# Gated-merge blocks staged in f32 in a later block's place, their split spaced by matmul columns, and the second gate's weights split ahead of the conv forms

## The chip, the core and the metric

One core of one Trainium2 chip runs the whole encoder block in one launch. The metric is the device time of the program in microseconds (us), as the median of repeated runs. The engines are called by the profile's names: PE is TensorE's matmul queue, PEld its weight loads, DVE is VectorE, ACT is ScalarE, POOL is GpSimd, and SP (SyncE) issues every DMA of the part that is told here. Each engine takes its instructions in the order of its own queue; semaphores tie the queues together.

## The reference, cut to what matters

```
u = RMSNorm(x)
[q|k|v|cB|cC|cH|gA|gB] = u @ W_in               # gA, gB: 1024 channels each
A   = neighbourhood_attention(q, k, v)          # 512 channels
B   = cB * conv3(cC * cH)                       # 512 channels
y_A = A @ W_A ;  y_B = B @ W_B                  # to 1024 channels each
m   = sigmoid(gA) * y_A + sigmoid(gB) * y_B     # per channel and token
x   = x + m @ W_o
x   = x + relu(RMSNorm(x) @ W1)^2 @ W2
```

There are 1024 tokens and 1024 channels, all in float32.

## The kernel before

Every f32 operand of a matmul is scaled by a power of two and split into two f16 halves, `hi` (ACT: a scaled copy) and `lo` (DVE: the scaled operand minus `hi`). A product is then three f16 matmuls. The scale of a weight chunk comes from its squares or its largest entry. ACT or DVE makes one column per chunk, DVE rounds it to bf16 (`sum_of`, L1173 and L1174, or `largest`, L389 and L391), PE sums it over the partitions with a 128x1 matmul on `ones` (`all_sum`, L231), and DVE reads the sum back (L234) and makes the scale with some five one-column operations (`pow2_half`, L490 to L497, or `pow2`). A chunk's column sum here always means that 128x1 matmul: it stands in PE's queue between products, so everything behind it waits until DVE has cast the column.

The change lies in the middle of the program, between the attention and the output projection. There the merged activations m are made in eight blocks n of 128 channels:

- Gate n (`gate_units`): the two gates' products for block n. For n from 1 to 7 they are made by a seven-product scheme (`seven`): seven units of 12 matmuls on sums of the weights' quarters ("forms", `gsum`, made by POOL in `forms_sum`, L1320) and on sums of the activations (`FORM`). A gate's four 512-token pieces live in a tile `sg`, of which there are two. The posts of a unit add the products into `sg` on DVE (L1463 to L1480), and one ACT sigmoid (L1474) ends the gate.
- Attention units (`a_unit`): one unit of 12 matmuls for half the tokens of a block; DVE multiplies the product into `sg` (L1515).
- Conv units (`ab`): blocks n = 2j and 2j+1 share seven units of 6 matmuls on forms of the conv branch. Those activations' forms are made once (`conv_late`: `hi`, L938; `lo`, L941), parked in `M`, written to DRAM (`bf`) and read back form by form into four slots (`land`, tile `bT`). DVE multiplies the products into `sg` (L1526).
- `join` adds both halves of a block on POOL (L1536); when both 512-token halves are in, `m_done` squares the block (ACT, L1436), makes a scale (DVE, L1438 and L490 to L497) and splits it into the two halves of `M` (ACT L1441, DVE L1443). `M` is a pair of tiles of eight blocks each, `mH` and `mL`, and is what the output projection reads.

The weights of gate n are prepared by `prep_s(n)` (tile `w_s`: ACT L1338 for `hi`, DVE L1334 for `lo`), those of the conv branch by `prep_b(j)` (`w_wb`, same lines), those of the attention branch by `prep` (`w_wa`, L362 and L349). The raw weights come through five buffers (`raw`, L264 on SP), each loaded again when its last reader is through.

The order of all this on the engines is made when the program is built. `unit` writes a unit's matmuls and then advances background work: `tick` steps the list `bg` (weight preparations), `step` steps `fg` (forms, splits of m). A preparation spaces its own steps by `apart`, which waits until a number of matmul columns (`work`; one unit of 12 is 6144) has been written. `built` drives both lists until a chunk's weights are split.

```
def apart(mark, n=3, of=units):
    while of[0] < mark + n and not forced[0]:
        yield WAIT
```

Of the kernel before, what the change touches and what calls it, by code (L numbers as in the profile page):

```python
# [101 lines left out]
def encoder_block(ctx: ExitStack, tc: tile.TileContext, x, weights, cols, gqk, rel, masks, out):  # L102
# [28 lines left out]
    area = {"keep": [0, 0, 144], "prep": [144, 144, 240], "tmp": [240, 240, 512]}  # L131
# [814 lines left out]
    def conv_late():  # L946

        zs = zb.rearrange("p n t -> p (n t)").bitcast(F16).rearrange("p (n w t) -> p n w t", n=4, w=2)
        ms = [M[i][:, 2 + n].rearrange("p (w t) -> p w t", w=2) for i in range(2) for n in range(6 - 2 * i)]
# [236 lines left out]
    def aged(ch, i):  # L1186
        return forced[0] or i >= len(ch.when) or work[0] >= ch.when[i] + 2 * 6144
# [154 lines left out]
    def forms_split(ch, t, s, P):  # L1342
# [6 lines left out]
        todo = [(0, 1, r[0][:, 0:1]), (1, 3, r[1]), (3, 5, t[:, 0:2]), (5, 7, t[:, 2:4])]  # L1349
        yield from parts([((lambda i, a=a, b=b: P[:, a:b, i]), w) for a, b, w in todo], s, then)  # L1350
# [3 lines left out]
    def prep_s(n):  # L1354
# [6 lines left out]
        else:  # L1361
            yield from rows_scaled(ch, g1)
            sm = yield from squares(ch, M[1][:, 7].bitcast(BF16))
# [15 lines left out]
    def prep_b(j):  # L1379
# [7 lines left out]
        for a in range(2):  # L1387
            A.activation(M[1][:, 6, :512].bitcast(BF16), raw[:, 512 * a:512 * a + 512], AF.Square,
# [40 lines left out]

    def m_done(n):  # L1430

        m = sgs[n][:, 0::2]
        hi, lo = (M[w][:, n].rearrange("p (h t) -> p h t", h=2) for w in range(2))
        ss, s = tmp(), tmp()
        yield
        A.activation(lo.bitcast(BF16), m, AF.Square, accum_out=sc[:, ss])  # L1436
        yield
        V.tensor_scalar(sc[:, ss], sc[:, ss], 1e-36, None, op0=OP.max)  # L1438
        yield
        yield from pow2_half(ss, 14, s, at(rowsM, n))  # L1440
        A.activation(hi, m, AF.Copy, scale=sc[:, s])  # L1441
        yield
        V.scalar_tensor_tensor(lo, m, sc[:, s], hi, op0=OP.mult, op1=OP.subtract)  # L1443
        merged.add(n)

    def gate_units(n, tail=None):
# [24 lines left out]
        def post3(ps):  # L1471
# [3 lines left out]
            if tail:  # L1475
                tail(sg, 0)
        seven(cS[n].P, actS, 0, 512, {
            1: lambda ps: A.activation(z[0], ps[1], AF.Copy),
            6: lambda ps: V.tensor_tensor(z[1], ps[6], z[0], op=OP.add),
            2: lambda ps: V.tensor_tensor(z[0], ps[2], z[0], op=OP.add),  # L1480
            5 if n == 1 else 7: post7, 3: post3}, 2, 5 if n < 7 else 6, (1, 6, 2, 4, 7, 5, 3) if n == 1 else (1, 6, 2, 4, 5, 7, 3))
# [795 lines left out]
```

## Time and profile before

| | |
|---|---|
| median of 3 runs (lowest to highest) | 1222.78 us (1222.61 to 1223.08) |
| the profiled execution's own time | 1222.02 us |
| span of its profile | 1220.2 us |
| mean granted PE clock | 0.994 |
| PE busy | 1191.6 us, 98% of the span |
| DVE busy | 959.1 us, 79% |
| ACT busy | 777.6 us, 64% |
| POOL busy | 479.9 us, 39% |

Times in the rows of the profile are us from the start of the span. A row of the timeline gives the start, the length, the engine (with q for its sequencer), the line of the kernel, the operation, what is written and read, and in brackets how long the engine had been idle before it and what released it. The chip's DMA engines carry out what SP issues: a DMA row on SP is the issue, not the transfer.

### The profile page before, as it was taken

How to read it: one execution, taken by the hardware profiler on the slowest of the kernel's cores; microseconds unless marked ns; L12 is line 12 of the kernel's file. 1: busy time of each engine (PE TensorE's matmuls, PEld its weight loads, DVE VectorE, ACT ScalarE, POOL GpSimd, SP SyncE). 2: the span in 40 equal slices, each digit the busy share in tenths (PEclk: the TensorE clock that was granted, in tenths of full speed). 3: DMA queues.
4: the chain of work that ended last, by engine and by line, in shares of the span. 5: the costliest groups of instructions: out<-in, count | busy, mean ns of one | idle time of the engine just before them, and what ended most of it. 6: DMA issues, size and time to landing. Idle time of an engine off the chain costs nothing.

```text
span 1220.2 us, 17138 instructions
## 1 busy us (share of the span) xinstructions
PE 1191.6 (98%) x6248; PEld 573.6 (47%) x6248; DVE 959.1 (79%) x1793; ACT 777.6 (64%) x1241; POOL 479.9 (39%) x314
## 2 busy tenths in 40 slices
PE   8999999999897998999999999999999999999998
PEld 7444444545343443444458444444444444444444
DVE  7987778898787867876878665555448989999998
ACT  7775668778665745335768887687776754646430
POOL 5610021121433341401003665755657563464472
PEclk9999999999899999999999999999999999999999
DMA  7755555777583423316096654354384934436212
GB/s 264 201 152 114 110 112 116 154 157 136 140 303 126 154 71 121 104 71 258 18 176 153 207 190 148 137 190 153 133 293 164 345 129 156 174 113 231 96 43 104
DMA packets 168373, 189.62 MB, mean 155 GB/s; under 512 B 123616, under 2 KB 124128, under 8 KB 164192
## 3 DMA queue, kind: packets, MB, share of 16 engines
q1 hardware_dynamic: 168288, 188.52, 51.4%
q8 instruction: 49, 0.80, 0.3%
q14 instruction: 36, 0.29, 0.1%
HBM read 117.19 MB, written 41.42 MB: 130 GB/s over the span
## 4 chain that ended last, share of the span: by engine, by line
PE 79%; DVE 12%; ACT 4%; POOL 2%; issue 2%; DMA 2%; DVEq 0%; ACTq 0%; POOLq 0%
PE ps_d L240 23%; PE ps_s L240 19%; PE ps_o L240 17%; PE ps_d L1161 10%; DVE w_s L1334 2%; PE ps_d L690 2%; PE ps_d L739 2%; PE ps_s L739 2%; DVE w_wb L1334 2%; PE ps_s L690 1%; PE ps_o L1142 1%; PE ps_s L1066 1%; DMA raw<-in_weights 1%; POOL sg L1536 1%; DVE sc L381 1%
## 5 line engine op out<-in xcount | busy, mean ns | idle before, releaser
L240 PEld LDWEIGHTS <-ops 128*128 128x128 f16 x1356 | 132.5, 98 | 157.3
L240 PEld LDWEIGHTS <-w 128*128 128x128 f16 x1368 | 132.8, 98 | 139.5
L1161 PE MATMUL ps_d<-uT,w_ws 128*128 128x512 f16 x576 | 127.9, 379 | 0.0
L240 PE MATMUL ps_s<-ops 128*128 128x512 f16 (+1 forms) x528 | 119.7, 377 | 0.0
L240 PE MATMUL ps_d<-ops 128*128 128x512 f16 x480 | 110.1, 379 | 0.0
L2098 ACT ACTIVATE ops<-hf,sc 128x2048 f16<-128x2048 f32 x26 | 52.0, 1998 | 84.8 <-PE ps_s L240 37.7
L1320 POOL TENSOR_TENSOR tsum<-raw 128x512 f32<-128x512 f32 x28 | 48.2, 1740 | 139.4 <-DVE v L1726 74.7
L1676 POOL TENSOR_TENSOR as<-as 128x512 f32<-128x512 f32 x60 | 83.0, 1383 | 41.6 <-ACT as L1958 38.0
L240 PEld LDWEIGHTS <-w_s 128*128 128x128 f16 x588 | 57.8, 100 | 87.1 <-issue 16.2
L1161 PEld LDWEIGHTS <-w_ws 128*128 128x128 f16 x576 | 54.5, 98 | 65.1 <-issue 1.0
L240 PE MATMUL ps_d<-u2T,w 128*128 128x512 f16 (+1 forms) x360 | 78.8, 368 | 0.0
L240 PE MATMUL ps_o<-ops 128*128 128x512 f16 (+1 forms) x348 | 78.6, 375 | 0.0
L2100 DVE SCALAR_TENSOR_TENSOR ops<-hf,sc,ops 128x2048 f16<-128x2048 f32 x26 | 74.2, 2852 | 3.2 <-ACT ops L2098 2.2
L240 PE MATMUL ps_o<-u2T,w 128*128 128x512 f16 (+1 forms) x348 | 76.0, 368 | 0.0
L240 PE MATMUL ps_s<-u2x,w 128*128 128x512 f16 (+1 forms) x336 | 74.5, 371 | 0.0
L1196 ACT ACTIVATE raw<-raw,sc 128x256 f32<-128x256 f32 x164 | 67.8, 494 | 7.2 <-DMA raw<-in_weights 7.2
L1536 POOL TENSOR_TENSOR sg<-sg 128x512 f32<-128x512 f32 x14 | 20.4, 1466 | 95.7 <-DVE sg L1515 55.6
L1338 ACT ACTIVATE w<-raw,sc 128x512 f16<-128x512 f32 (+1 forms) x28 | 24.6, 927 | 50.5 <-DVE sc L496 50.5
L1991 DVE TENSOR_TENSOR as<-ps_s,as 128x512 f32<-128x512 f32 x13 | 9.0, 692 | 57.9 <-ACT as L2010 57.9
L2114 POOL TENSOR_TENSOR raw<-raw 128x1024 f32<-128x1024 f32 x8 | 30.8, 3873 | 36.8 <-DVE ops L2108 36.8
L240 PEld LDWEIGHTS <-mH 128*128 128x128 f16 x304 | 29.6, 98 | 30.8 <-issue 0.3
L2104 ACT ACTIVATE ops<-raw,sc 128x1024 f16<-128x1024 f32 x24 | 26.3, 1138 | 26.6 <-DVE sc L152 19.2
(429 smaller groups left out, 2734.6 us busy)
## 6 DMA issues: line engine op xcount, KB each, us to landing
raw<-in_weights SPq DMA_DIRECT2D x89, 512.0 KB, 5.8
hs<-as SPq DMA_DIRECT2D x16, 1792.0 KB, 7.9
hf<-hs SPq DMA_DIRECT2D x26, 1024.0 KB, 6.4
bT<-bf SPq DMA_DIRECT2D x28, 512.0 KB, 4.9
w2x<-in_weights SPq DMA_DIRECT2D x16, 512.0 KB, 7.6
raw<-in_weights SPq DMA_DIRECT2D x16, 384.0 KB, 3.6
xt<-in_x SPq DMA_DIRECT2D x8, 512.0 KB, 10.6
gs<-s SPq DMA_DIRECT2D x4, 1024.0 KB, 4.5
```

Source lines behind the costliest of these rows:

```text
L240: T.matmul(ps, l, r, start=a, stop=b)
L690: T.matmul(ps, UT[:, sa, k, b * 128:(b + 1) * 128], w, start=(kind, k) == ("hh", 0), stop=(kind, k) == ("hl", 7))
L739: T.matmul(vbank["q", b], UT[:, sa, k, b * 128:(b + 1) * 128], cQ.parts[:, sw, 512 * k:512 * k + 512], start=(k, n) == (0, 0), stop=(k, n) ...
L1161: T.matmul(ps, l, r, start=a, stop=b)
L1196: A.activation(v, v, AF.Copy, scale=sc[:, at(g, 4 * i + k)])
L1320: G.tensor_tensor(t[:, o], a, b, op=OP.add)
L1334: V.scalar_tensor_tensor(o(1), w, sc[:, scale(n - 1)], o(0), op0=OP.mult, op1=OP.subtract)
L1536: G.tensor_tensor(t, t, part(n, 2 * half + 1), op=OP.add)
L1676: sub.tensor_tensor(z[o], z[a], z[b], op=op)
L2098: A.activation(P[:, 1, 0], hf, AF.Copy, scale=sc[:, Rs])
L2100: V.scalar_tensor_tensor(P[:, 1, 1], hf, sc[:, Rs], P[:, 1, 0], op0=OP.mult, op1=OP.subtract)
L2114: G.tensor_tensor(w11[i2], w11[i2], w12[i2], op=OP.add)
```

## The change

1. A finished block n below 6 is no longer joined in `sg`. POOL writes the sum in f32 to `whole(n)`: two neighbouring 1024-column places of `mH` (even n) or `mL` (odd n), those of blocks n+1 and n+2, which are written later. So `sg` is free after the joins, and the two loops that stepped until block n-2 was split, ahead of a gate, are gone.
2. `m_done` reads that place and spaces its four steps (square, scale, `hi`, `lo`) one unit (6144 columns) apart, and it waits for the block before it. Scale columns are kept (`sums`, `scales`) and not taken from a ring. A loop before the output projection forces what is left.
3. The weights of gate 1 are put ahead of the conv forms and of `prep_b(0)` in the lists, without the wait of a unit, and with the last two pairs of forms in the other order. Gate 1's units run in the order 1, 2, 6, 4, 7, 5, 3 (before 1, 6, 2, 4, 7, 5, 3).
4. `built` first tries up to 12 plain steps before it forces. The first raw weights of gate 2 are used 4 units after their load, not 2.
5. Scratch outputs of squares move from `mL` to `mH`, and the parking of the conv forms is spread 5 and 5 over `mH` and `mL` (it was 6 and 4).

```diff
@@ built
+        for _ in range(12):
+            if all(ch.split for ch in chs):
+                return
+            tick()
+            step()
         forced[0] = True
...
@@ aged
-        return forced[0] or i >= len(ch.when) or work[0] >= ch.when[i] + 2 * 6144
+        return forced[0] or i >= len(ch.when) or work[0] >= ch.when[i] + (4 if ch is cS[2] else 2) * 6144
...
@@ prep_s, forms_split
+        if turned:
+            todo[2:] = todo[:1:-1]
...
-        yield from apart(work[0], 6144, work)
+        if n > 1:
+            yield from apart(work[0], 6144, work)
...
-        yield from forms_split(ch, t, s, ch.P)
+        yield from forms_split(ch, t, s, ch.P, n == 1)
...
+    def whole(n):
+        return M[n % 2][:, n + 1:n + 3].rearrange("p n t -> p (n t)").bitcast(F32)
...
@@ m_done
+        if n < 6:
+            m, gap = whole(n), 6144
+        else:
+            m, gap = sgs[n][:, 0::2], 0
+            hi, lo = (t.rearrange("p (h t) -> p h t", h=2) for t in (hi, lo))
+        while n and n - 1 not in merged:
+            yield WAIT
+        yield from apart(work[0], gap, work)
         A.activation(lo.bitcast(BF16), m, AF.Square, accum_out=sc[:, ss])
         yield
+        yield from apart(work[0], gap, work)
         V.tensor_scalar(sc[:, ss], sc[:, ss], 1e-36, None, op0=OP.max)
         yield
+        s = at(scales, n)
         yield from pow2_half(ss, 14, s, at(rowsM, n))
+        yield from apart(work[0], gap, work)
         A.activation(hi, m, AF.Copy, scale=sc[:, s])
         yield
+        yield from apart(work[0], gap, work)
         V.scalar_tensor_tensor(lo, m, sc[:, s], hi, op0=OP.mult, op1=OP.subtract)
...
@@ join
-            G.tensor_tensor(t, t, part(n, 2 * half + 1), op=OP.add)
+            o = whole(n)[:, 512 * half:512 * half + 512] if n < 6 else t
+            G.tensor_tensor(o, t, part(n, 2 * half + 1), op=OP.add)
...
@@ the order of the stage
     tick(8)
+    bg.append(prep_s(1))
+    tick(2)
     fg.append(first_forms())
-    bg.extend([prep_b(0), prep_s(1)])
+    bg.append(prep_b(0))
...
             built(cS[n])
-            while j and n - 2 not in merged:
-                step()
             sgs[n] = gate_units(n)
...
         settle()
-        while n - 2 not in merged:
-            step()
         sgs[n] = gate_units(n)
```

What moves is shown at three places. Rows of the kernel before carry its line numbers; those of the changed kernel stand 5 to 31 lines further on for the same code.

First, ACT's queue from the split of the first attention weights (`w_wa`) on, at the start of this stage. `w_s` are the split weights of gate 1, `zb`, `mH` and `mL` from `bT` are the conv forms' `hi`, and `sg` from `raw` and `ps_o` are the sigmoids of gate 0. Before:

```order
L362 ACTIVATE w_wa<-raw,sc 128x256 x4
L938 ACTIVATE zb<-bT 128x512 x3
L1388 ACTIVATE mL,sc<-raw,sc 128x512 x2
L1196 ACTIVATE raw<-raw,sc 128x2x128 x4
L938 ACTIVATE mH<-bT 128x512 x3
L1457 ACT_TABLE_LOAD
L1457 ACTIVATE sg<-raw 128x512
L1454 ACTIVATE sg<-ps_o,sc 128x512
L938 ACTIVATE zb<-bT 128x512
L938 ACTIVATE mH<-bT 128x512
L1338 ACTIVATE w_s<-raw,sc 128x512
```

The same stretch of ACT's queue now:

```order
L367 ACTIVATE w_wa<-raw,sc 128x256 x4
L1343 ACTIVATE w_s<-raw,sc 128x512
L1343 ACTIVATE w_s<-raw,sc 128x2x512
L943 ACTIVATE zb<-bT 128x512 x3
L1343 ACTIVATE w_s<-gsum,sc 128x2x512 x2
L943 ACTIVATE mH<-bT 128x512 x2
L943 ACTIVATE mL<-bT 128x512
L1396 ACTIVATE mH,sc<-raw,sc 128x512 x2
L1481 ACT_TABLE_LOAD
```

All four `hi` of gate 1 now stand ahead of the sigmoids of gate 0, and the scaling of gate 2's raw weights (L1196, now L1201) has gone behind them. On SP two raw loads moved with this from behind eight DMA transposes (`uT` from `gs`) to ahead of them. On PE no product changes its place beyond the order of gate 1's units, but the column sums of the attention weights A1 and of gate 2's weights stand two units earlier. After the fifth unit of gate 1 stood the sum of A1:

```order
L240 MATMUL ps_d<-qD,w_s 128x512
L231 LDWEIGHTS ones
L231 MATMUL ps_s<-ones 128x1
L240 LDWEIGHTS w_s
L240 MATMUL ps_o<-uT,w_s 128x512
```

At the same place now stands the sum of gate 2's weights, that of A1 being two units further up:

```order
L245 MATMUL ps_s<-qD,w_s 128x512
L236 LDWEIGHTS ones
L236 MATMUL ps_o<-ones 128x1
L245 LDWEIGHTS w_s
L245 MATMUL ps_d<-uT,w_s 128x512
```

Second, DVE's queue behind the first pair of blocks, that is behind `ab(0)`, beside gate 2. L1526 is the last multiplication into `sg`; L1438 begins the scale of a block of m, L1173 and L1174 cast a weight chunk's column, L234 reads a column sum. Before:

```order
L1526 SCALAR_TENSOR_TENSOR sg<-zb,sc,sg 128x512
L1438 TENSOR_SCALAR sc<-sc 128x1
L490 TENSOR_SCALAR sc<-sc 128x1
L492 TENSOR_SCALAR sc<-sc 128x1
L1438 TENSOR_SCALAR sc<-sc 128x1
L494 TENSOR_SCALAR sc<-sc 128x1
L490 TENSOR_SCALAR sc<-sc 128x1
L496 TENSOR_SCALAR sc<-sc 128x1
L497 TENSOR_SCALAR sc<-sc 128x1
L492 TENSOR_SCALAR sc<-sc 128x1
L494 TENSOR_SCALAR sc<-sc 128x1
L1443 SCALAR_TENSOR_TENSOR mL<-sg,sc,mH 128x1024
```

The same stretch of DVE's queue now:

```order
L1556 SCALAR_TENSOR_TENSOR sg<-zb,sc,sg 128x512
L1178 TENSOR_REDUCE sc<-sc 128x1
L1179 CAST ones<-sc 128x1
L1459 TENSOR_SCALAR sc<-sc 128x1
L239 TENSOR_SCALAR sc<-ps_o 128x1
L495 TENSOR_SCALAR sc<-sc 128x1 x2
L497 TENSOR_SCALAR sc<-sc 128x1
L499 TENSOR_SCALAR sc<-sc 128x1
L501 TENSOR_SCALAR sc<-sc 128x1
L502 TENSOR_SCALAR sc<-sc 128x1
L1505 TENSOR_TENSOR sg<-ps_d,sg 128x512
```

Before, both blocks' scales and both `lo` (two L1443) stood ahead of the next cast and of gate 3's scale; now the cast is first and gate 3's scale (L239 on) follows the first step of block 0 alone.

Third, ACT's queue beside gate 4, behind the scaling and squares of gate 6's raw weights. `w_s` are gate 5's weights here. Before:

```order
L1436 ACTIVATE mL,sc<-sg 128x1024
L1441 ACTIVATE mH<-sg,sc 128x1024
L1436 ACTIVATE mL,sc<-sg 128x1024
L1338 ACTIVATE w_s<-raw,sc 128x512
L1338 ACTIVATE w_s<-raw,sc 128x2x512
L1338 ACTIVATE w_s<-gsum,sc 128x2x512 x2
L1478 ACTIVATE sg<-ps_d 128x512
```

The same stretch of ACT's queue now:

```order
L1456 ACTIVATE mL,sc<-mH 128x1024
L1343 ACTIVATE w_s<-raw,sc 128x512
L1343 ACTIVATE w_s<-raw,sc 128x2x512
L1343 ACTIVATE w_s<-gsum,sc 128x2x512 x2
L1509 ACTIVATE sg<-ps_d 128x512
L1343 ACTIVATE w_wb<-raw,sc 128x128
```

The square of block 3 (the second L1436) stood between block 2's and gate 5's split; it now stands behind that split, with six instructions between.

More of the change, by code (lines that the diff above doesn't have):

```diff
@@ L948, in conv_late @@
         zs = zb.rearrange("p n t -> p (n t)").bitcast(F16).rearrange("p (n w t) -> p n w t", n=4, w=2)
-        ms = [M[i][:, 2 + n].rearrange("p (w t) -> p w t", w=2) for i in range(2) for n in range(6 - 2 * i)]
+        ms = [M[i][:, 2 + n].rearrange("p (w t) -> p w t", w=2) for i in range(2) for n in range(5)]
         st = [[zs[:, n] for n in range(4)] + ms[:3], ms[3:10]]
@@ L1362, in prep_s @@
             yield from rows_scaled(ch, g1)
-            sm = yield from squares(ch, M[1][:, 7].bitcast(BF16))
+            sm = yield from squares(ch, M[0][:, 7].bitcast(BF16))
             yield from apart(work[0], 2 * 6144, work)
@@ L1387, in prep_b @@
         for a in range(2):
[L1388 removed]
+            A.activation(M[0][:, 7, :512].bitcast(BF16), raw[:, 512 * a:512 * a + 512], AF.Square,
                          scale=sc[:, at(rowsB, a)], accum_out=sc[:, at(sm, a)])
@@ L1621, in encoder_block @@
     settle()
+    forced[0] = True
+    while len(merged) < 7:
+        tick()
+        step()
+    forced[0] = False
     drain()
```

22 lines of the change are left out of this document (13 added, 9 removed).

## The prediction

> **What bounds the kernel now.** I read the page's busy times, then PE's waits, then its clock and busy time by stage.
>
> ```profile
> span 1220.2 us, 17138 instructions
> PE 1191.6 (98%) x6248; PEld 573.6 (47%) x6248; DVE 959.1 (79%) x1793; ACT 777.6 (64%) x1241; POOL 479.9 (39%) x314
> ```
>
> ```profile
> PE ps_d L231 <- DVE ones L391: 5.2, 1, 5.2
> PE ps_s L231 <- DVE ones L1174: 3.5, 2, 3.2
> PE ps_d L240 <- DMA bT<-bf: 3.0, 1, 3.0
> PE ps_s L240 <- DVE sc L234: 2.4, 1, 2.4
> ...
> PE ps_s L240 <- ACT w_s L1338: 2.0, 1, 2.0
> PE ps_s L240 <- DVE w_s L1334: 1.6, 1, 1.6
> ...
> PE ps_d L240 <- DVE w_s L1334: 0.9, 1, 0.9
> ```
>
> ```profile
> 300.00:340.00 40.00, 35.55 (x167) 15.41 (x166) 28.68 (x47) 26.86 (x49) 13.19 (x10) 0.91 0.66 169
> 340.00:400.00 60.00, 51.97 (x238) 23.04 (x236) 48.92 (x116) 36.03 (x63) 23.75 (x20) 0.97 0.54 190
> 400.00:460.00 60.00, 57.53 (x270) 25.92 (x269) 43.16 (x96) 35.58 (x66) 23.79 (x20) 1.00 0.36 114
> 460.00:520.00 60.00, 54.89 (x250) 24.61 (x250) 47.72 (x93) 27.78 (x43) 16.57 (x14) 0.97 0.38 121
> 520.00:580.00 60.00, 59.74 (x281) 27.05 (x279) 44.28 (x82) 28.78 (x49) 7.63 (x6) 1.00 0.42 160
> ```
>
> PE is the bound almost everywhere: 28.6 us of the span are idle. Of these, 20.3 lie in the changed stage (4.45 + 8.03 + 2.47 + 5.11 + 0.26 from the five stretches), and there the granted clock falls to 0.91 and 0.97. No single engine is full in that stage: DVE is the busiest and is idle 11 us of 340 to 400. So PE waits on chains through the queues of DVE, ACT and POOL, and a wait that goes is worth only as much as the chain behind it gets shorter.
>
> **Part 1: gate 1's weights first.** PE at gate 1 and at the last conv unit behind it:
>
> ```profile
> 329.79 4.45 PE L240 MATMUL ps_s<-uT,w_s 128*128 128x512 f16 x10 [1.58 <-DVE w_s L1334]
> ...
> 338.16 2.75 PE L240 MATMUL ps_s<-uT,w_s 128*128 128x512 f16 x12
> 340.75 2.75 PE L240 MATMUL ps_o<-uT,w_s 128*128 128x512 f16 x12
> ...
> 367.69 1.47 PE L240 MATMUL ps_d<-bT,w_wb 128*128 128x512 f16 x6 [2.97 <-DMA bT<-bf]
> ```
>
> A unit takes 2.59 us (340.75 − 338.16). The change puts all `lo` of `w_s` ahead of gate 1, so its waits of 2.0, 1.6 and 0.9 go, and with them the slow clock: ten matmuls in 4.45 where 10/12 of 2.59 are 2.16 (2.1 to 2.3 more). That is 6.7 us at most. What is late next is DVE:
>
> ```profile
> 311.25 5.19 DVE L349 SCALAR_TENSOR_TENSOR w_wa<-raw,sc,w_wa 128x256 f16<-128x256 f32 x4 [2.81 <-ACT w_wa L362]
> ...
> 322.38 0.69 DVE L941 TENSOR_TENSOR mH<-bT,mH 128x512 f16<-128x512 f32 x1 [2.08 <-ACT mH L938]
> ...
> 344.67 0.16 DVE L1174 CAST ones<-sc 128x1 bf16<-128x1 f32 x1
> ...
> 354.79 0.68 DVE L1472 TENSOR_TENSOR sg<-ps_d,sg 128x512 f32<-128x512 f32 x1
> ...
> 415.24 1.68 DVE L349 SCALAR_TENSOR_TENSOR w_wa<-raw,sc,w_wa 128x256 f16<-128x256 f32 x4
> ```
>
> ```profile
> 355.50 2.00 ACT L1474 ACTIVATE sg<-sg,sc 128x2048 f32<-128x2048 f32 x1 [7.39 <-DVE sg L1472]
> ```
>
> ```profile
> 359.44 1.92 SPq L264 DMA_DIRECT2D raw<-in_weights  x2
> 361.45 0.38 SPq L1489 DMA_DIRECT2D bT<-bf  x1
> ```
>
> From 311 to 355.5 DVE's own queue is the path, nearly without a gap. Behind it hangs a tail: L1472 releases the sigmoid on ACT (L1474), which stands ahead of the split of gate 2's weights. That split frees two raw buffers, for which two raw loads block SP's queue (359.44), and behind these stands the `bT` load (361.45) for which PE waits until 367.69. The change leaves every link of this tail where it is, so what counts is when DVE ends L1472. It loses the wait of 2.08. It gains the scale of A1, five one-column operations that stood behind L1472 and now stand ahead of it (at the 0.16 of the cast, about 0.85). The work beside POOL changes too: four 128x256 operations take 5.19 beside POOL's sums and 1.68 alone, 0.88 more each, and one to two more operations of `w_s` now lie there (0.9 to 1.8). Sum −0.3 to +0.6, and I take 0: DVE is at L1472 when it was before, and the `bT` load comes at 367.7 again.
>
> PE therefore gains nothing by 367.7. It would be ready 6 us early, and waits instead at two places: at the column sum of gate 2's weights, now ahead of the sixth unit of gate 1 (gate 1 would begin at 329.8 − 1.6 − 2.0, less 0.6 for its first two matmuls, that is 325.6; the column sum ahead of it now waits 1 us for a cast behind `w_s`; 5 × 2.59 later PE is at 339.6, and the cast of 344.67 comes 2.1 − 0.9 = 1.2 earlier: 4 us), and longer at the `bT` load. The SP queue: two raw loads now stand ahead of eight transposes and block until `w_s` is split (about 320), so the forms' writes begin about where they did. Reach of this part: −6.7 if the tail breaks, +3 if ACT is late for DVE.
>
> The Trainium skill (SBUF — State Buffer, Who interferes with whom) says that a DVE operation with two SBUF inputs and a GpSimd operation that reads SBUF exclude each other for the whole instruction. The trace's 5.19 against 1.68 agrees with that in kind; a full POOL operation for each moved `lo` would put L1472 about 1 us later, and the whole forecast by as much.
>
> **Part 2: the splits of blocks 0 and 1.**
>
> ```profile
> 379.21 0.15 DVE L1438 TENSOR_SCALAR sc<-sc 128x1 f32<-128x1 f32 x1 [2.73 <-ACT mL L1436]
> ...
> 385.14 0.16 DVE L1174 CAST ones<-sc 128x1 bf16<-128x1 f32 x1
> 385.21 0.15 DVE L234 TENSOR_SCALAR sc<-ps_o 128x1 f32<-128x1 f32 x1
> ...
> 389.39 2.48 DVE L1334 SCALAR_TENSOR_TENSOR w_s<-gsum,sc,w_s 128x1024 f16<-128x1024 f32 x2
> ```
>
> ```profile
> 380.06 3.47 POOL L1320 TENSOR_TENSOR gsum<-gsum,raw 128x512 f32<-128x512 f32 x2
> 387.10 4.13 PE L240 MATMUL ps_s<-qD,w_s 128*128 128x512 f16 x12
> ```
>
> DVE stands 2.73 us ahead of 379.21, then works through two `lo` that each wait for ACT, and only at 385.14 casts the column for which PE has stood 3.2 us (1.6 more for the next one), after which 12 matmuls take 4.13 and not 2.75 (1.4). In the new order the cast comes first, and gate 3's scale follows the first step of block 0, for which nothing but block 0's square is needed: it starts before 379.2 − 2.7 + 0.5, about 377, not at 385.21. Its split is then held by POOL's `gsum`, which end at 383.5, and ends at about 386 in place of 391.9. So PE's 3.2 + 1.6 + 1.4 = 6.2 go. Against that I set 1.5 for a slow clock after the longer `bT` wait of Part 1 (like the 1.4 here). At gate 3 PE is 4.7 ahead. DVE is not: both `lo` (1.24 each, as L1334 at the same 128x1024) leave the place where PE stood and come back later in its queue, so that by gate 4 PE is stopped by PSUM banks that DVE has not yet read, and keeps some 2.5.
>
> **Part 3: block 3's square.**
>
> ```profile
> 435.30 3.54 POOL L1320 TENSOR_TENSOR gsum<-raw 128x512 f32<-128x512 f32 x2
> 442.67 1.06 ACT L1436 ACTIVATE mL<-sg 128x1024 bf16<-128x1024 f32 x1 [6.34 <-POOL sg L1536]
> 443.73 1.75 ACT L1338 ACTIVATE w_s<-raw,sc 128x512 f16<-128x512 f32 x2
> ...
> 446.71 2.47 DVE L1334 SCALAR_TENSOR_TENSOR w_s<-gsum,sc,w_s 128x1024 f16<-128x1024 f32 x2
> ```
>
> ```profile
> 464.90 0.16 DVE L391 CAST ones<-sc 128x1 bf16<-128x1 f32 x1
> 465.13 4.36 PE L240 MATMUL ps_s<-uT,w_s 128*128 128x512 f16 x12
> 474.23 0.16 DVE L1174 CAST ones<-sc 128x1 bf16<-128x1 f32 x1
> ```
>
> ACT stands 6.34 us for the join of block 3, which POOL has queued behind gate 5's `gsum`, and gate 5's split stands behind it on ACT; DVE's whole queue waits with it. The change puts the square behind the split. POOL's third join ahead of the `gsum` waits for DVE's last pieces of that block; these stood behind block 2's scale steps, which wait for ACT's square of it, and stand ahead of them now. With the 2.5 of Part 2 the join and so the `gsum` begin some 4 earlier (431 for 435.30) and end at about 437; the split of gate 5 then ends at about 439.6 in place of 449.2: 9.5 earlier. From there to the cast of 464.90 the queue of DVE keeps its order but for some 0.6 of steps of m that move, so the cast comes at about 456, 8.9 earlier. Of PE's waits of 2.4 and 5.2 and the slow 4.36 (1.6), 9.2 together, 2 to 3 stay as shorter waits at this cast and the next (474.23, also about 9 earlier). From then on PE had no wait of a microsecond in this stage, and everything behind moves as a block.
>
> **Sum.** 0 (Part 1) + 2.5 (Part 2 after what DVE takes back) + 6.4 (Part 3) = 8.9, less 0.4 for the joins of block 4 and the `lo` that now fall beside PE's run: 8.5. The profiled execution's 1222.02 becomes 1213.5. It lies 0.76 below the median of the runs, so the median becomes 1214.3. A difference under 0.2% (2.4 us) cannot be told from none here.
>
> **The rivals.**
>
> *More: the tail of Part 1 shortens too.* If DVE, rid of the 2.08 and with `w_s` behind it, reaches L1472 some 4 us earlier, the sigmoid, both raw loads and the `bT` load do too, and up to 6.7 − 4 for the new column sum plus the 3.0 at 367.69 count: some 6 more, 1208. For it: 5.19 against 1.68 shows how much POOL's overlap costs, and the overlap could fall better. Against it: the same POOL work meets the same DVE work. Chance 0.13.
>
> *Less: the columns hold.* The casts L391 and L1174 near 465 depend on gate 4's posts and gate 5's sigmoid as well. If these and not block 3's square are what is late, 464.90 moves by 2.5 only, and the median is 1219.5. Against it: between gate 5's split and that cast DVE's queue keeps its order, and the split itself stood behind that square. Chance 0.14.
>
> *Nothing to be told.* The new waits eat it all, within 2.4 of 1222.8. Chance 0.06.
>
> *Slower: a spaced square meets a join that isn't there.* A step is now placed by matmul columns, not by POOL. Where POOL is later than the columns say, ACT stands at L1436 as it does for 6.34 now, but in front of work that is needed sooner: block 3's square now stands between the two halves of a `w_wb` split, block 5's ahead of gate 7's. Two such stops of 6.3 for the 8.9 taken away are 1222.8 + 3.7 = 1226.5. It decides as soon as joins come more than about 6 us later than in my walk (block 3's at 438.5, its square's turn at 444.5). Chance 0.17.
>
> *My forecast*, 6 to 11 us gained, has 0.50.
>
> **How the numbers follow.** The range takes the forecast's own 1211.5 to 1217, the rival with more (1208, and 1 to 2 us of unknown in it) and the one with less: 1206 to 1221; slower and most of the unchanged case stay out. Faster by over 0.2%: 0.50 + 0.13 + 0.14 = 0.77. Within: 0.06. Slower: 0.17.
>
> **What would show it.** Right: no wait of gate 1 for `w_s`; a wait of about 4 us for a cast L1179 inside gate 1; the `bT` wait near 367 still there, and longer; no wait for a cast in gate 2; gate 5's split on ACT right behind block 2's square; the cast L396 near 456. Wrong: the `bT` load well before 366 (more), an ACT wait of several us at L1456 (slower), or the cast L396 after 462 (less).

## The result: 1216.05 us, 0.57% faster, and the profile after

| | before | after |
|---|---|---|
| median (lowest to highest), 4 runs each | 1222.69 us (1222.54 to 1223.08) | 1216.05 us (1214.99 to 1216.23) |
| ratio, 95% interval | | 0.9943 [0.9926, 0.9961] |
| the profiled execution's own time, span | 1222.02 us, 1220.2 us | 1214.99 us, 1213.2 us |

The medians differ by 6.6 us, the profiled executions by 7.0. The page of the changed kernel begins with these busy times:

```profile
span 1213.2 us, 17139 instructions
PE 1191.6 (98%) x6248; PEld 574.6 (47%) x6248; DVE 962.0 (79%) x1793; ACT 777.8 (64%) x1241; POOL 482.3 (40%) x314
```

PE's busy time is what it was, to the tenth; the whole gain is idle time. PE's largest waits (engine, line, what it waited for: total, times, longest), and then the five stretches of the stage (start to end, length, busy time of PE, PEld, DVE, ACT and POOL with the number of instructions, granted clock, DMA share, GB/s):

```profile
PE ps_d L245 <- DMA bT<-bf: 5.0, 1, 5.0
PE ps_o L236 <- DVE ones L1179: 3.6, 1, 3.6
PE ps_d L236 <- DVE ones L396: 3.6, 1, 3.6
```

```profile
300.00:340.00 40.00, 38.45 (x195) 17.71 (x194) 30.78 (x58) 27.33 (x50) 13.65 (x10) 1.00 0.77 188
340.00:400.00 60.00, 51.31 (x223) 22.34 (x222) 49.09 (x110) 38.34 (x71) 26.30 (x23) 0.91 0.50 178
400.00:460.00 60.00, 56.42 (x266) 25.50 (x264) 48.47 (x100) 33.63 (x59) 24.88 (x18) 1.00 0.38 123
460.00:520.00 60.00, 60.00 (x274) 26.94 (x273) 50.49 (x94) 29.88 (x46) 15.26 (x13) 0.98 0.44 141
520.00:580.00 60.00, 59.96 (x282) 27.23 (x280) 43.28 (x87) 31.18 (x54) 7.04 (x6) 1.00 0.37 141
```

PE's idle time in the stage is now 1.55 + 8.69 + 3.58 + 0 + 0.04 = 13.9 us, 6.4 less than the 20.3 of before. The first stretch has lost its waits for `w_s` (4.45 to 1.55), but the second is no better (8.03 to 8.69) and its clock is lower (0.91 for 0.97). The gain shows from 400 on. How PE's lead over the old kernel comes about is seen by laying PE's timeline against that of before. The second product of gate 2 and one of the first of gate 4, before:

```profile
371.61 2.75 PE L240 MATMUL ps_d<-qD,w_s 128*128 128x512 f16 x12
...
444.26 2.75 PE L240 MATMUL ps_d<-qD,w_s 128*128 128x512 f16 x12
```

The same two places after, with the rows at which PE stood idle or was slow, now or before:

```profile
344.16 0.16 PE L236 MATMUL ps_o<-ones 128*128 128x1 bf16 x1 [3.65 <-DVE ones L1179]
...
368.89 2.74 PE L245 MATMUL ps_d<-bT,w_wb 128*128 128x512 f16 x6 [5.04 <-DMA bT<-bf]
371.42 4.14 PE L245 MATMUL ps_s<-uT,w_s 128*128 128x512 f16 x12
...
375.43 2.75 PE L245 MATMUL ps_d<-qD,w_s 128*128 128x512 f16 x12
...
388.43 2.75 PE L245 MATMUL ps_o<-s4T,w_s 128*128 128x512 f16 x12
...
441.62 2.75 PE L245 MATMUL ps_d<-qD,w_s 128*128 128x512 f16 x12
...
458.32 0.16 PE L236 MATMUL ps_d<-ones 128*128 128x1 bf16 x1 [3.58 <-DVE ones L396]
458.34 4.12 PE L245 MATMUL ps_s<-uT,w_s 128*128 128x512 f16 x12
```

PE is 3.8 us behind the old kernel at gate 2 (375.43 for 371.61), and 2.64 ahead at gate 4 (441.62 for 444.26). At the sum that waited 5.2 us before it now stops for 3.58 and goes on 6.8 ahead (458.34 for 465.13). In the span it is 7.0.

### The profile page after: what moved, and what is told of

It reads as the page before. It is cut to its first block, busy times and chain, and to the rows that moved or that the text cites. A ratio compares the mean times of both kernels' runs of the same rounds, so it can differ in the third digit from the quotient of the medians.

```text
span 1213.2 us, 17139 instructions
## 1 busy us (share of the span) xinstructions
PE 1191.6 (98%) x6248; PEld 574.6 (47%) x6248; DVE 962.0 (79%) x1793; ACT 777.8 (64%) x1241; POOL 482.3 (40%) x314
## 4 chain that ended last, share of the span: by engine, by line
PE 87%; DVE 8%; ACT 2%; issue 1%; POOL 1%; DMA 1%; DVEq 0%; ACTq 0%; POOLq 0%
PE ps_d L245 26%; PE ps_s L245 23%; PE ps_o L245 19%; PE ps_d L1166 9%; PE ps_d L695 2%; PE ps_d L744 2%; PE ps_s L744 2%; DVE w_s L1339 2%; PE ps_s L695 2%; PE ps_o L1147 1%; PE ps_s L1071 1%; POOL gsum L1325 1%; DVE w_wb L1339 1%; ACT raw L1201 1%; DMA bT<-bf 1%
## 5 line engine op out<-in xcount | busy, mean ns | idle before, releaser
L1201 ACT ACTIVATE raw<-raw,sc 128x256 f32<-128x256 f32 x164 | 67.8, 493 | 1.9 <-DMA raw<-in_weights 1.9
L2106 POOL TENSOR_TENSOR t<-raw,w2x 128x1024 f32<-128x1024 f32 x6 | 18.7, 3114 | 62.0 <-DMA w2x<-in_weights 62.0
```

Source lines behind the costliest of these rows:

```text
L1201: A.activation(v, v, AF.Copy, scale=sc[:, at(g, 4 * i + k)])
```

## The experiments

Times are medians; the ratio is to the kernel before, run on the same chip at the same time (1223.1 to 1223.4 us).

### Gate 1's weights alone

The kernel before with Part 1 alone: weights of gate 1 ahead of the conv forms, order of units, order of the pairs, age of gate 2's raw weights, the plain steps of `built`. Blocks of m stay as they were.

```diff
     tick(8)
+    bg.append(prep_s(1))
+    tick(2)
     fg.append(first_forms())
-    bg.extend([prep_b(0), prep_s(1)])
+    bg.append(prep_b(0))
```

> The kernel before with Part 1 alone (gate 1's weights ahead of the conv forms, its units in the new order, the older raw weights for gate 2); blocks of m as before. My theory (the time saved in gate 1 only turns into longer waits): no wait of gate 1 for w_s, a wait of about 3.6 us for a cast inside gate 1 and of about 5 us for the bT load, PE at the second unit of gate 2 near 375.4 (before 371.6), then hardly a wait for gate 2's casts, since these stand in DVE's queue behind blocks 0 and 1 at about 385 to 388 as before, the wait of about 5 us for A3's cast near 465 unchanged: 1222.7 us, 1221.5 to 1223.7. Rival (gate 1's 4.5 us of waits and 2.2 of slow clock were on the path): 1216 to 1218.

Measured: 1224.58 us, ratio 1.001 [1.0001, 1.0019]. PE's timeline in this kernel:

```profile
387.22 0.16 PE L236 MATMUL ps_s<-ones 128*128 128x1 bf16 x1 [3.35 <-DVE sc L239]
```

The wait inside gate 1 is there (3.66 us, at 344.92), and what was saved in gate 1 is gone by gate 3. The total lies a little above the range expected: the `bT` wait was shorter (3.09 us), but at gate 3, where hardly a wait was expected, PE stands 3.35 and then 1.56 (388.94). Part 1 by itself gains nothing.

### The spacing alone

The changed kernel without Part 1: the lines of the first experiment's diff reversed, with `aged`, `forms_split` and the order of gate 1's units as before.

> The changed kernel without Part 1 (gate 1's weights, unit order and raw weights of gate 2 as before); blocks of m wait in f32 and are spaced. My theory (all of the gain is in Parts 2 and 3): gate 1 waits 4.5 us for w_s, the bT wait near 367.7 is 3 us with no slow clock behind it, gate 2's casts come without a wait, gate 3 starts 1 to 3 us earlier than in the changed kernel, the cast of A3 near 456 to 458: 1214.5 us, 1213 to 1216.5, so no slower than the changed kernel. Rival (Part 1 gives its share, the two add): 1218 to 1220.

Measured: 1216.12 us, ratio 0.994 [0.9927, 0.9952], the same as the whole change. The sum that waits for the cast near 458 comes 0.8 us later than in the changed kernel, which the median does not show:

```profile
459.14 0.16 PE L236 MATMUL ps_d<-ones 128*128 128x1 bf16 x1 [4.63 <-DVE ones L396]
```

The two runs together settle Part 1: the gain is that of Parts 2 and 3. The plain steps of `built` stand in both kernels, and the moved scratch places (point 5) only in the second; neither was tried by itself.

### The conv form's load ahead of the raw loads

In the changed kernel, the `bT` load for which PE waits 5.04 us is issued ahead of the two raw loads that block SP's queue. Nothing else moves.

```diff
-        while pend and (forced[0] or pend[0][0] <= work[0]):
+        while pend and not hold[0] and (forced[0] or pend[0][0] <= work[0]):
...
-            ps[i] = anybank()
+            ps[i], hold[0] = anybank(), j == 0 and o in (2,)
...
-            land(7 * j + o + 4)
+            land(7 * j + o + 4); hold[0] = False; due() if j == 0 else None
```

> The changed kernel, but the one bT load for which PE waits near 368.9 is issued on SP ahead of the two raw loads that block its queue from 356 to 362.5 and not behind them; nothing else moves on any engine. My theory (the raw loads in front of it are the tail): the load is issued near 357.5 and the wait of 5.0 us and the 2.6 us of slow clock behind it go; a wait of up to 3 us for the cast of 370.45 comes in their place, gate 3 starts some 3 us earlier, and DVE's and POOL's queues let 1 to 4 us of it through to the end: 1213 us, 1211.5 to 1215. Rival A (behind gate 2 DVE's queue sets the time and eats all of it): 1216 us. Rival B (the slot of that load comes free late by itself, so its place on SP doesn't matter): the wait stays near 5 us, 1216 us. Rival C (all 7.6 us reach the end): 1208.5 us.

Measured: 1216.17 us, ratio 0.9941 [0.9929, 0.9954]: no gain. PE's timeline:

```profile
363.82 1.46 PE L245 MATMUL ps_d<-bT,w_wb 128*128 128x512 f16 x6
...
371.38 0.16 PE L236 MATMUL ps_o<-ones 128*128 128x1 bf16 x1 [3.50 <-DVE ones L1179]
373.31 4.67 PE L245 MATMUL ps_d<-qD,w_s 128*128 128x512 f16 x12 [1.77 <-DVE zb L1582]
```

The product on `bT` runs at 363.82 with no wait, 5.07 earlier. The next column sum then waits 3.50 for its cast and the next product 1.77 for a bank that DVE has not read: 5.27. With the slow matmuls behind them (4.67) PE is where it was, at 385.59 for 385.79 at the next sum, as rival A had it. The load was late, but DVE's queue behind it was as late; that is why Part 1, which does not shorten that queue, gains nothing.

### Blocks 2 and 3 unspaced

The changed kernel with the four steps of blocks 2 and 3 directly behind one another, so that block 3's square stands ahead of gate 5's split again.

```diff
-            m, gap = whole(n), 6144
+            m, gap = whole(n), 0 if n in (2, 3) else 6144
```

> The changed kernel with the steps of blocks 2 and 3 not spaced: block 3's square stands on ACT behind the first of four pieces of gate 5's split again, and not behind all of them. My theory (Part 3 is that square): ACT stands there some 6 us for POOL's join behind the gsum, gate 5's split ends near 447 in place of 441.8, the cast of A3 comes near 463 in place of 458.1 and PE's wait for it grows from 3.6 to about 6 to 8 us, with a wait for gate 5's scale before it: 1220.5 us, 1218.5 to 1222. The four gsum of gate 5, beside which DVE then stands still, take about 6.2 us as before and not 7.6, if what lengthened them is DVE's split beside them. Rival (the posts of gate 4 and the conv split hold that cast): 1216 to 1217.

Measured: 1223.52 us, ratio 1.0003 [0.9994, 1.0012], above the range expected. All of the gain is gone, Part 2's too. ACT and PE in this kernel:

```profile
442.37 1.06 ACT L1456 ACTIVATE mL<-mL 128x1024 bf16<-128x1024 f32 x1 [7.06 <-POOL mL L1567]
```

```profile
465.94 0.16 PE L236 MATMUL ps_d<-ones 128*128 128x1 bf16 x1 [6.97 <-DVE ones L396]
```

ACT's stop of 6.34 is back as one of 7.06, at the square of block 3, and the sum that follows is at 465.94, later than the 465.1 of before. The lead of gates 2 and 3 is eaten by a wait of 6.97 at the same cast. So the parts are not terms to be added: block 3's square is the gate through which any earlier lead must pass. (Block 2's steps were closed up with block 3's; the edit does not part the two.) Gate 5's four `gsum` took 6.5 us here (434.62 to 441.12), less than 7.5 but not 6.2: DVE did not stand still beside them, it had one `lo` of block 2 and one of `w_s` to do (2.19 at 434.79, 1.75 at 436.90).

### Blocks 0 and 1 as before

The changed kernel with blocks 0 and 1 unspaced and finished ahead of gates 2 and 3, as the loops that were taken out did. Blocks 2 and 3 stay spaced.

```diff
-            m, gap = whole(n), 6144
+            m, gap = whole(n), 0 if n < 2 else 6144
...
-            built(cS[n])
+            built(cS[n]); [step() for _ in range(99) if n == 3 and 1 not in merged]
...
-        settle()
+        settle(); [step() for _ in range(99) if n == 2 and 0 not in merged]
```

> The changed kernel with the steps of blocks 0 and 1 close together again and forced ahead of gates 2 and 3, as before; blocks 2 to 5 stay spaced. My theory (Part 2 is real, and what PE is ahead at gate 3 reaches the end, since gate 5's gsum start behind posts that PE releases): both lo stand ahead of gate 3's split on DVE again, which ends near 390 and not at 387.5, PE waits 1 to 3 us at gate 3, the gsum of gate 5 begin 1 to 3 us later than 431.7 and the cast of A3 follows: 1218 us, 1216.8 to 1220. Rival (the chain behind block 3's square sets the time alone, and PE's lead before it is lost): 1216 us.

Measured: 1218.42 us, ratio 0.9962 [0.995, 0.9975]. That is 2.4 us above the changed kernel's median (1.9 by the differences to each one's own runs of before), and every run of it is above every run of the changed kernel. POOL and PE:

```profile
434.33 1.73 POOL L1325 TENSOR_TENSOR gsum<-raw 128x512 f32<-128x512 f32 x1
```

```profile
460.92 0.16 PE L236 MATMUL ps_d<-ones 128*128 128x1 bf16 x1 [5.83 <-DVE ones L396]
```

Gate 5's `gsum` begins at 434.33, 2.6 later than in the changed kernel (431.73, shown below), and the cast comes 2.6 later: Part 2's lead goes through POOL's joins to that split, one for one.

### Taking away the waits that are left

Three kernels ask what the waits still shown are worth. The first puts the column sums of the fourth attention weights and of the last `w_wb` two units later on PE, so that the cast near 458 is not yet needed:

```diff
-                yield from apart(work[0], 3 * 6144, work)
+                yield from apart(work[0], {3: 5}.get(cA.index(self), 3) * 6144, work)
...
-        s, ch.inv = yield from scale_of(am, 0, 3 if j else 2)
+        s, ch.inv = yield from scale_of(am, 0, (2, 3, 3, 5)[j])
```

> The changed kernel with two column sums on PE put two units later: that of the last attention weights (cast near 458.1, weights needed only some 60 us later) and that of the last conv weights (cast near 467.4). My theory (these are the last places where PE waits for DVE's queue in this stage, for work that nobody needs yet): the wait of 3.6 us at 458, the slow clock behind it (1.3 and 0.4) go and no wait as long takes their place: 1211.5 us, 1210.5 to 1213. Rival (DVE's posts are as late as its casts; PE runs into PSUM banks not yet read, or into weights of gate 6 not yet split): 1214 to 1216.

Measured: 1215.7 us, ratio 0.9938 [0.9926, 0.9951]. The wait of 3.58 is gone, and PE waits for banks and for a later cast instead:

```profile
455.69 4.44 PE L245 MATMUL ps_d<-uT,w_s 128*128 128x512 f16 x12 [2.02 <-DVE sg L1487]
...
471.99 1.24 PE L245 MATMUL ps_d<-qD,w_wa 128*128 128x512 f16 x5 [1.47 <-DVE sg L1487]
...
482.76 0.18 PE L236 MATMUL ps_d<-ones 128*128 128x1 bf16 x1 [1.55 <-DVE ones L1179]
```

2.02 + 1.47 + 1.55 = 5.0 us of waits for DVE, in the place of 3.58.

The second adds to the load put first (above) that the split of the second attention weights starts 4 units later, which frees DVE for the cast near 371:

```diff
-            f = o = 0
+            f = o = 0; yield from apart(work[0], 24576 if self.kind == 'A' and self is cA[1] else 0, work)
```

> The kernel with the bT load first, and the split of the second attention weights (2.7 us of DVE at 365.8, needed only near 411) put on DVE and ACT behind the last products of blocks 0 and 1. In the run with the load first PE waited 3.5 us for a cast at 371.4, 1.8 us for a PSUM bank and lost 2 us to a slow clock, since that split and the posts stood ahead of the cast on DVE. My theory (DVE's queue from 356 to 375 is what holds PE there): cast and posts come 2.7 to 3.3 us earlier, PE is at the second unit of gate 2 near 370 and without the slow clock at 377.8 some 4 us earlier; about half of it reaches the end through gate 5's gsum: 1213.5 us, 1212 to 1215. Rival (the time behind it is set by POOL and ACT and not by PE's or DVE's earlier start): 1216 us.

Measured: 1215.72 us, ratio 0.994 [0.9927, 0.9952]. PE reaches the second sum of gate 2 at 381.11, 4.7 earlier than the changed kernel (385.8), and loses it to DVE again: from there to 481 the trace has seven waits for DVE, of 0.45 us and more, 8.6 us in all, where the changed kernel has the one of 3.58. The longest:

```profile
480.52 0.16 PE L236 MATMUL ps_s<-ones 128*128 128x1 bf16 x1 [2.19 <-DVE ones L1179]
```

The third has both edits.

> The edits of the last two together: bT load first, split of the second attention weights later, two column sums two units later. My theory: the gains add, 1209 us, 1207 to 1211.5. Rival (one bound behind the other, the second edit makes room only for what the first has shown): no faster than the better of the two alone, 1211.5 to 1214.

Measured: 1215.48 us, ratio 0.9938 [0.9924, 0.9952]. That is above the theory's range and the rival's. None of the three differs from the changed kernel by more than the intervals allow, where some 2.5 to 7 us less had been expected. I had taken each named wait for the cause; it is where DVE's lateness surfaces. Moving PE's need for a cast does not make DVE earlier: in these rows it is DVE's queue that sets the time, up to 480 at least. The rival of the second kernel, that POOL and ACT set it, names the same time; that it is DVE rests on what released PE in these rows, and on the next kernels.

### One thing that makes DVE late: the work beside POOL

In the changed kernel, DVE beside gate 4 and 5, and then POOL:

```profile
431.57 2.96 DVE L1339 SCALAR_TENSOR_TENSOR w_s<-raw,sc,w_s 128x512 f16<-128x512 f32 x2
...
440.49 1.28 DVE L1339 SCALAR_TENSOR_TENSOR w_s<-gsum,sc,w_s 128x1024 f16<-128x1024 f32 x1 [2.34 <-ACT w_s L1343]
...
449.91 3.94 DVE L1339 SCALAR_TENSOR_TENSOR w_wb<-raw,sc,w_wb 128x256 f16<-128x256 f32 x3 [0.30 <-ACT w_wb L1343]
...
458.11 0.16 DVE L396 CAST ones<-sc 128x1 bf16<-128x1 f32 x1
```

```profile
431.73 3.93 POOL L1325 TENSOR_TENSOR gsum<-raw 128x512 f32<-128x512 f32 x2
435.61 3.66 POOL L1325 TENSOR_TENSOR gsum<-gsum,raw 128x512 f32<-128x512 f32 x2
...
449.29 2.87 POOL L1325 TENSOR_TENSOR gsum<-raw 128x512 f32<-128x512 f32 x2
452.12 2.85 POOL L1325 TENSOR_TENSOR gsum<-gsum,raw 128x512 f32<-128x512 f32 x2
```

Four `gsum` beside DVE's `lo` take 431.73 to 439.27, 7.54 us. Three `lo` of `w_wb` beside the next `gsum` take 3.94. A first attempt to part the two was meant to hold gate 5's first `lo` back in the program's order, until the `gsum` were done:

```diff
-            if prev:
+            if prev and hold5 and n < 4:
+                kept.append(prev)
...
+                for o, w in kept + [prev]:
```

> The changed kernel, but DVE writes the four lo of gate 5's split only when all four hi are there, so that nothing of that split stands beside the gsum of gate 5 on POOL. This isolates what lengthened them from 6.2 to 7.6 us. If DVE's operations beside them do (my theory): the four gsum take 5.0 to 5.8 us and end near 437; DVE then writes the four lo in one piece, ends near 443 in place of 441.8, and the cast of A3 comes 0.5 to 1.5 us later: 1217 us, 1216 to 1218. Rival (the gsum are slow by themselves at that place, from their sources or from DMA traffic): they take over 7 us again, and the time is 1218 to 1219.

Measured: 1214.99 us (1214.95 to 1216.21), ratio 0.9934 [0.9921, 0.9948]. It does not test the theory: on DVE no other work stood between these `lo`, so the instructions came out in the same order on every engine. It is a repeat of the changed kernel, and its spread of 1.3 us shows how far a difference must go to be read.

Two kernels hold an engine by data instead. The first makes POOL wait, ahead of gate 6's `gsum`, for DVE's last `lo` of `w_wb`, with one addition of a single column:

```diff
+        if ch is cS[6]: G.tensor_tensor(sc[:, tmp()], PB[2][:, 6, 1, 255:256], PB[2][:, 6, 1, 255:256], op=OP.add)
```

> The changed kernel with one 128x1 addition on POOL ahead of the four gsum of gate 6; it reads the last piece of the conv weights' split, so that these sums start only when DVE is through with that split. The sums move from 449.3 to about 453; they are needed near 463. Theory (DVE's queue holds PE at 458, and POOL beside it makes the 128x256 pieces last 1.2 us each where they take 0.5 alone): the four pieces behind 448.7 take 2.3 to 3 us in place of 4.8, the cast of A3 comes near 456, PE's wait of 3.6 falls to 1.5 and the slow clock behind it goes: 1213.3 us, 1212 to 1215. Rival A (POOL is then late for gate 6's split or for the joins of blocks 4 and 5): 1216 to 1218. Rival B (what PE gains there it waits for at the next cast, near 467): 1215 to 1216.

Measured: 1213.62 us (1213.31 to 1213.78), ratio 0.992 [0.9906, 0.9933]; not one of its runs is as slow as the fastest of the repeat above, which ran beside it (the intervals of the two ratios overlap). DVE, POOL and PE:

```profile
451.52 1.28 DVE L1340 SCALAR_TENSOR_TENSOR w_wb<-raw,sc,w_wb 128x256 f16<-128x256 f32 x3 [0.29 <-ACT w_wb L1344]
```

```profile
452.88 0.19 POOL L1324 TENSOR_TENSOR sc<-w_wb 128x1 f32<-128x1 f16 x1 [1.94 <-DVE w_wb L1340]
453.03 2.49 POOL L1326 TENSOR_TENSOR gsum<-raw 128x512 f32<-128x512 f32 x2
455.47 2.61 POOL L1326 TENSOR_TENSOR gsum<-gsum,raw 128x512 f32<-128x512 f32 x2
```

```profile
457.27 0.16 PE L236 MATMUL ps_d<-ones 128*128 128x1 bf16 x1 [3.18 <-DVE ones L396]
457.30 2.75 PE L245 MATMUL ps_s<-uT,w_s 128*128 128x512 f16 x12
```

The three `lo` take 1.28 for 3.94, and DVE is through with them 1.05 us earlier although they start 1.6 later; by so much gate 5's `gsum` were late in this execution already (433.34), ahead of the edit. PE's sum comes 1.05 earlier, at 457.27. Its wait fell to 3.18 only, not to 1.5: the cast came at 457.06 and not near 456, and PE came 0.65 sooner too. But a unit at full speed follows it, so that PE is 2.7 ahead of the changed kernel at 462.47 (465.21 there). Of this it waits 1.37 at the next cast (466.60), as rival B had it, and 1.2 reaches the end of the span. POOL starts its sums 3.7 later (453.03) and ends them 3.1 later (458.08), which nothing on PE feels. This shows the contention, and what it cost DVE here: 2.66 us on three operations.

The second adds to that the later column sums of above.

> The edit of the last one together with the two column sums put two units later. In the run with the sums alone PE met PSUM banks that DVE had not read yet (waits of 2.0 at 455.7, with a slow clock behind it, and of 1.5 at 472 and 482). Theory (DVE's posts are the bound there, and 2 us less in front of them come through): 1212.5 us, 1211 to 1214.5. Rival (the banks wait for other posts): 1215 to 1216.

Measured: 1213.05 us (1212.36 to 1213.32), ratio 0.9915 [0.9902, 0.9929]: the fastest kernel here, ahead of both the kernel before and the changed one. Against the held POOL alone, whose runs it overlaps by a hundredth, its 0.6 us is not told apart.

The last also makes DVE wait for gate 5's `gsum`, with one column read from the last of them:

```diff
+        if ch is cS[5]: V.tensor_scalar(sc[:, tmp()], t[:, 3, 511:512], 1e-30, None, op0=OP.max)
```

> The kernel with POOL held and the two sums later, and one 128x1 operation on DVE ahead of the four lo of gate 5's split; it reads the last of gate 5's gsum, so that nothing of the split runs on DVE beside them (the edit that was to do this before left every row where it was). Theory (DVE's operations beside them lengthened the gsum from 6.2 to 7.6 us): the four gsum take 5.0 to 5.5 us, all four lo come behind them in 4.5 us, so that the split ends within 0.7 us of where it did, and the time stays: 1213 us, 1212 to 1214. Rival (the gsum are slow there by themselves): 7.5 us again, the split ends 2 us later, 1215 us.

Measured: 1213.52 us (1212.4 to 1214.78), ratio 0.9921 [0.9907, 0.9934]. POOL, then DVE:

```profile
433.05 2.49 POOL L1326 TENSOR_TENSOR gsum<-raw 128x512 f32<-128x512 f32 x2
435.49 2.61 POOL L1326 TENSOR_TENSOR gsum<-gsum,raw 128x512 f32<-128x512 f32 x2
```

```profile
438.14 0.15 DVE L1358 TENSOR_SCALAR sc<-gsum 128x1 f32<-128x1 f32 x1 [5.36 <-POOL gsum L1326]
438.27 2.80 DVE L1340 SCALAR_TENSOR_TENSOR w_s<-raw,sc,w_s 128x512 f16<-128x512 f32 x2
441.00 2.47 DVE L1340 SCALAR_TENSOR_TENSOR w_s<-gsum,sc,w_s 128x1024 f16<-128x1024 f32 x2
```

Alone, the four `gsum` take 5.05 us (433.05 to 438.10); 7.54 was the price of company. But DVE, which stood 5.36 for it, then has the `lo` still to do, the first of them beside POOL again (a join of 1.27 from 438.06), and ends the split 10.4 us after the `gsum` began (443.47), where in the changed kernel it was 10.0 (441.77). Here the overlap costs as much as it saves, and the time does not change.

The contention also falls differently from one execution to the next. Six of the kernels (the changed one, its repeat, the two sums later, POOL held, both of these, and DVE held) have the same instructions in the same order on every engine up to gate 5's split near 431. Yet in their traces DVE ended gate 3's split at 387.60, 387.66, 388.77, 389.23, 388.10 and 388.92, and gate 5's `gsum` began 44.1 us behind that end in each (431.73 to 433.34). In the three late ones DVE came to that split soonest (380.00 to 380.34, for 380.56 to 381.54), and POOL took 7.35 to 7.48 us for the `gsum` beside it, for 5.39 to 6.38. So a difference of up to 1.6 us between two of these traces, ahead of 431, need not come from an edit.

## Why the prediction came out, and where it did not

The total came out 1.8 us above the forecast (1216.05 for 1214.3), with the gain where it was argued to be. The largest term was too large by 2.2 us, and another held, in the execution that was profiled, only because two errors in it cancelled.

**Part 1, forecast 0.** Right, and shown by three runs. The waits for `w_s` went; the new wait inside gate 1 is 3.65 (4 forecast); the `bT` wait is still there, and longer. Off in size: the `bT` product came at 368.89 and not again at 367.69. DVE ended the step that releases the sigmoid 1.1 us later. The step read before as L1472 is L1496 now; DVE, and then SP with the issue of the `bT` load, in the changed kernel:

```profile
355.90 0.68 DVE L1496 TENSOR_TENSOR sg<-ps_s,sg 128x512 f32<-128x512 f32 x1
```

```profile
362.56 0.38 SPq L1519 DMA_DIRECT2D bT<-bf  x1
```

Before they stood at 354.79 and 361.45: both ends of the tail are 1.1 later, outside the −0.3 to +0.6 of the sum. What failed is that DVE's queue alone is the path from 311 to 355.5. The wait of 2.08 went, and DVE was 1.66 ahead where it reads the sum of `w_wb` (339.05 for 340.71). There it stands for ACT's first `hi` of `w_wb`, 2.07 where it was 0.47: that `hi` began at 341.86 for 341.90, since ACT now scales gate 2's raw weights just ahead of it. At 351.16 DVE was level with before (351.20), and the 1.1 is the scale of A1, which took 1.15 (0.85 in the sum). The variant worked out beside the Trainium skill, about 1 us later, had the size right for another reason: by 351 nothing was left of what the moved `lo` cost. The slow clock behind the `bT` wait cost 2.6 (six matmuls in 2.53 and a unit in 3.98, from 368.89 to 371.42 and 375.40, where 1.30 and 2.59 are full speed) for the 1.5 set aside. A slow unit stood behind the new wait in gate 1 too (344.26 to 348.15, 3.89), for which no term stood. None of this mattered: PE was 3.8 late at gate 2, and DVE, not PE, carried the time on from there, as the load put first shows.

**Part 2, forecast 2.5, measured 2.6.** The casts come at 376.5 and 379.2, far ahead of PE, and the 6.2 are gone. The split of gate 3 ended late:

```profile
381.54 3.67 DVE L1339 SCALAR_TENSOR_TENSOR w_s<-raw,sc,w_s 128x512 f16<-128x512 f32 x2
385.13 2.47 DVE L1339 SCALAR_TENSOR_TENSOR w_s<-gsum,sc,w_s 128x1024 f16<-128x1024 f32 x2
```

It ended at 387.60, not 386: its first two `lo`, beside POOL's `gsum`, took 3.67, where before they took 1.94 (387.53) while POOL stood still. PE was 2.6 ahead at gate 3 (388.43 for 391.06), not 4.7. What I took off, a stop at a PSUM bank by gate 4 that would leave 2.5, did not come: it was 2.64 ahead still at 441.62. The lead was forecast too large, and so was the loss; that they cancelled is luck, and belongs to this execution. In the three late traces named above no slow clock followed the `bT` wait (2.50 to 2.74 us there): PE was 4.8 to 5.3 ahead at gate 3, stopped 0.81 for a bank near 425, and was 3.4 to 3.8 ahead at gate 4.

**Part 3, forecast 6.4, measured 4.2** (6.8 ahead at 458.32 less the 2.64 of gate 4). The mechanism is the one named, as the kernel with blocks 2 and 3 unspaced shows. The term that was mis-sized is the length of gate 5's `gsum`. They began at 431.73, as forecast (431), but I let them end at 437, with the length they had in the trace before, where DVE, but for one `lo` of block 2 (436.43), stood still for want of ACT. In the new order DVE has `lo` to do beside them: they took 7.54 and ended at 439.27. The split ended at 441.77 for 439.6 and the cast came at 458.1 for 456, all late by the same 2. So of the 9.2 of waits and slow clock there, 3.58 and a slow unit of 4.12 stayed (5.0), not 2 to 3. I had used that very contention in Part 1, 5.19 against 1.68, and not asked for it in Part 3. Nor was the 437 to be had by holding DVE back: in the last kernel above the `gsum` took 5.05, and the split came no sooner.

**The rest, forecast −0.4.** Nothing was lost behind the cast: 6.8 there, 7.0 in the span. 0 + 2.6 + 4.2 + 0.2 = 7.0, where 8.5 stood.

**The rivals.** The tail of Part 1 did not shorten (the `bT` product came at 368.89, not before 366), and the cast came at 458.1, not after 462. The slower case needed ACT to stand at a spaced square for about 6 us, and that sign came, at block 4:

```profile
489.19 1.06 ACT L1456 ACTIVATE mL<-mH 128x1024 bf16<-128x1024 f32 x1 [9.51 <-POOL mH L1567]
```

It cost nothing: at the same square ACT had stood 10.38 before (495.65), and PE ran without a gap beside both. The sign was named too widely, since a stop counts only where PE soon needs what stands behind it. At the other spaced squares, among them those of blocks 3 and 5 that the rival named, ACT's longest wait is 1.01 us (428.85): there the joins kept ahead of the columns. In the case with less, the 1219.5 is the profiled execution's time less 2.5; as a median it would have been 1220.3.

Open: why Part 1 alone is 0.1% slower, what decides how soon DVE comes to gate 3's split, and whether the small differences among the kernels with later sums (0.3 to 0.6 us) are anything.

## What to carry to other kernels

When a wait is taken from the engine that bounds, ask what the engine that released it would do next and whether that is on time: here three named waits of 3.5 to 5 us were removed and the time did not move, while one 0.19-us instruction that put four POOL operations 3.7 us later gained 1.4 over the repeat of the changed kernel. A duration read from a trace belongs to the company it ran in; when the order changes, so does the company, and both engines' rows in that place have to be costed anew. Parts of a change that feed the same queue aren't terms to be added: undo the last one on the path first.

## What was not expected of the hardware

**DVE and POOL, who pays.** Beside each other both lost, in different shares: POOL's four `gsum` went from 5.05 to 7.54 and DVE's two `lo` from 1.93 (at 405.05 in the changed kernel, with POOL idle) to 2.96; 18 us later DVE's three `lo` went from 1.28 to 3.94, and POOL's four from 5.05 to 5.68. The Trainium skill (SBUF — State Buffer, Who interferes with whom) says that a DVE instruction with two SBUF inputs contends with a GpSimd instruction that reads SBUF, as an exclusive lock, and that issue order decides who blocks. The rows agree that it can fall on either side. They do not bear out that the two never run together: one after the other the second pair would take 1.28 + 5.05 = 6.3, and it took 5.68.

**The clock after a wait.** The 3.18 us at 457.27 above were followed by a unit at full speed (2.75), but the 2.02 at 455.69, with the later sums, by one at near half (4.44). In the kernel with gate 1's weights alone:

```profile
468.06 0.16 PE L236 MATMUL ps_d<-ones 128*128 128x1 bf16 x1 [3.54 <-DVE ones L396]
468.09 2.75 PE L245 MATMUL ps_s<-uT,w_s 128*128 128x512 f16 x12
```

So the length of the wait does not decide it by itself, between 2.0 and 3.6 us at least. The Trainium skill (TensorE: Matmul & The Clock Gate, The HAM clock gate) has the clock halved after an idle window of about 3.4 us that runs freely; 2.02 us is less than such a window, and that row does not follow from it. What does decide was not tried.
